# A hybrid encoder layer: Up tiles in one piece of 512 columns, and the order of copies and lows in the turns

## The chip, the core and the metric

The kernel runs on one core of a Trainium2 chip. A core has engines that each work through a queue of their own: TensorE (PE in the profile, its weight loads apart as PEld), VectorE (DVE), ScalarE (ACT), GpSimd (POOL) and SyncE (SP, which here issues transfers only). They synchronise through semaphores. The metric is the device time of one execution in microseconds (us); the median of the runs shown stands for a kernel.

## The reference

One layer over 512 tokens of width 1024, in float32:

```python
x1 = x + rmsnorm(merged @ w_out, g_post_mix)          # merged: retention and SGU branches, gated
h2 = rmsnorm(x1, g_pre_ffn)                           # (512, 1024)
hid = h2 @ w_up                                       # (512, 5632): the Up product
hid = conv3_along_tokens(hid, conv_w) + conv_b        # depthwise
a, b = split(hid, 2)
y = x1 + rmsnorm((gelu(a) * b) @ w_down, g_post_ffn)  # w_down (2816, 1024): the Down product
```

Before it stand the input product (1024 to 8192 columns), a retention in both directions, a spatial gating unit and their output products.

## The kernel before

Every product is made of float32 operands split in two parts of a reduced format, high and low: ScalarE copies the high part (`copy`, line 80), VectorE subtracts it for the low part (line 87, 901). A product is then three matmuls, high x high, high x low, low x high (`mm3`, lines 218 to 221). Activations lie transposed, channels on partitions and the 512 tokens along the free axis; T0 and T1 are the two halves of 256 tokens. A weight block of 128 output channels by 1024 is read from a packed wall in DRAM by SP, split, and kept in one of nine slots (`slot`). The place of a slot's data is chosen by an offset in words: weights of Up blocks lie at 48 (high) and 16 (low) words past the start, activations 64 bytes past a multiple of 256. So Up's weights and its activations differ modulo 256 bytes, as in all stages with 256-wide matmuls but a few small ones; the stages with 512-wide matmuls have weights and activations at one place.

Some products use the Strassen-like scheme of class `Pair`: two output tiles from seven half products of 256 tokens (line 676), 84 matmuls of 256 columns, in three parts. Between the parts ordinary blocks are run, so that the sums on VectorE and ScalarE have time: `gated_pair` does it with two blocks of 512 columns (`f_block`), and the Up product does it in its eight *couples* of tiles, with two `up_block`s. An Up tile is two such blocks (the a and b channels of 128 hidden units each); of the 22 tiles, 0 and 1 are done early (`early`, four blocks), 2, 3, 20 and 21 by plain `up_block`s and 4 to 19 in couples. An `up_block` has 48 matmuls of 256 columns: first the eight k of T0, then, behind `between` (the third part of the Pair), the eight of T1. Early blocks do T0 of all four before T1.

h2 is made four times 128 tokens at a time. `norms(t)` has the residual and two row scales (statistics on ScalarE, a power on POOL, products on VectorE, line 870 to 882); `turn(t)` transposes its 8 pieces on TensorE (line 895) into two PSUM tiles and writes, for each quarter, the high part `h2h` (ScalarE), a raw copy `h2r` (ScalarE) and the low part `h2l` (VectorE). The raw copies serve `h2_sums`, whose results are the Pair's combined inputs. The order in which engines meet these instructions follows from the program's order and a scheduler; the accesses to one PSUM tile are made in program order. turn(0) and turn(1) lie between output products of `Down.finish`, turn(2) behind the first early block, turn(3) behind the fourth.

After Up, `down_forms` builds combined forms of the gated activations (fh, fl, fs, fa) and `products` multiplies them with combined weights, q and t units (dh, dl); `add_whole` handles four plain blocks that are left (`two_parts`, wh, wl). Before the loop over j, seven of the nine forms are built; two come later, in the loop.

Of the kernel before, what the change touches and what calls it, by code (L numbers as in the profile page):

```python
# [10 lines left out]
F32 = mybir.dt.float32  # L11
# [15 lines left out]
NW = 146  # L27
U0, GATE0, GATE1 = 32, 40, 72
LOOK = 4
NBLK = 76  # L30
WARM = 18
RES_OUT = 6
DOWN0 = NW - NF
# [15 lines left out]
def tile_block(ctx: ExitStack, tc, xT, x, wall, par, cs, wsp, bsp, gpost, gpre, gffn, out):  # L49
# [29 lines left out]
    def copy(o, i):  # L79
        nc.scalar.activation(out=o, in_=i, func=AF.Copy)  # L80

    def as32(t):
        return t.bitcast(F32)
# [152 lines left out]
    def col(i):  # L236
        return part[:, i : i + 1]

    xh, xl, xg = [], [], {}

    def load_x(k):
        t = tmp("xT")
        nc.sync.dma_start(t, xT[k])
        h_, l_ = blk(F32R, "xh"), blk(F32R, "xl")
# [598 lines left out]
    def row_scale(q):  # L843
# [7 lines left out]


    gpm, gpf = bcast(gpost, "gpm"), bcast(gpre, "gpr")
    h2h, h2l, h2r = ([[blk(dt, n) for _ in range(4)] for _ in range(2)]
                     for dt, n in ((F32R, "h2h"), (F32R, "h2l"), (F32, "h2r")))
    x1 = [[dp_.tile([P, S], F32, tag=f"x1_{t}{n}", name=f"x1_{t}{n}") for n in range(2)] for t in range(NT)]

    def norms(t, acc):

        xt = halves("x1")  # L860
        for n in range(2):
            nc.sync.dma_start(xt[n], x[t, :, n * S : (n + 1) * S])
        q = small("q", 2, 4)
        for n in range(2):
            mean_square(q, n, acc[n])
        sc, _ = row_scale(q)
        q = small("q", 2, 4)
        for n in range(2):
            z = tmp("z")
            v.scalar_tensor_tensor(  # L870
                out=z, in0=acc[n], scalar=sc, in1=gpm[n], op0=ALU.mult, op1=ALU.mult
            )
            v.tensor_add(xt[n], xt[n], z)
            mean_square(q, n, xt[n])
            nc.gpsimd.dma_start(x1[t][n], xt[n])
            if n == 0 and t in ADDED:
                nc.gpsimd.dma_start(out[t, :, 0:S], xt[0])
        sc, _ = row_scale(q)
        zs = []
        for n in range(2):  # L880
            z = tmp("xn")
            v.scalar_tensor_tensor(
                out=z, in0=xt[n], scalar=sc, in1=gpf[n], op0=ALU.mult, op1=ALU.mult
            )
            zs.append(z)
        return zs

    two = "p (i n) -> p i n"

    def turn(t, zs):  # L890
        g, c = t // 2, slice((t % 2) * P, (t % 2 + 1) * P)
        for n in range(2):
            p = ps()
            for f in range(4):
                nc.tensor.transpose(p[:, f * P : (f + 1) * P], zs[n][:, f * P : (f + 1) * P], ident)
            for i in range(2):
                hi, lo, raw = (h[g][2 * n + i].rearrange(two, i=2)[:, :, c] for h in (h2h, h2l, h2r))
                pf = p[:, 2 * i * P : 2 * (i + 1) * P].rearrange(two, i=2)
                copy(hi, pf)
                copy(raw, pf)  # L900
                v.tensor_sub(lo, pf, as32(hi))  # L901

    def h2(k, t):
        f = slice((k % 2) * 256, (k % 2 + 1) * 256)
        g = t.start // 256
        return h2h[g][k // 2][:, f], h2l[g][k // 2][:, f]

    h2forms = {n: [None] * 4 for n in ("S1", "S2", "S3", "S4")}

# [14 lines left out]
        for n, t in zip(("S1", "S2", "S3", "S4"), (b1, a0, a1, b0)):  # L924
            h2_parts(n, i, t)

    def h2_block(w, o, q):
# [12 lines left out]

    early_w, early_o = [], []

    def early(e, q):

        if q == 0:
            early_w.append(w_get(1))
            early_o.append(ps())
        h2_block(early_w[e], early_o[e], (T0, T1)[q])

    dn_ = Down(mh, ml, KD, RES_OUT)  # L950
    zs = {}
    for t in range(NT):
        acc = [dn_.finish(t, 0)]
        if t > 1:
            turn(t - 2, zs[t - 2])
        acc.append(dn_.finish(t, 1))
        zs[t] = norms(t, acc)
    early(0, 0)
    turn(2, zs[2])
    for e in range(1, EARLY):  # L960
        early(e, 0)
    turn(3, zs[3])
    for e in range(EARLY):
        early(e, 1)

# [20 lines left out]
        gp.append(blk(n="gp"))  # L986
        v.tensor_mul(gp[-1], ca, cb)  # L987

    def two_parts(t):
        h_, l_ = blk(F32R, "fh"), blk(F32R, "fl")  # L990
        split(h_, l_, t)
        return h_, l_

    def down_forms(j):
# [110 lines left out]
        M6: lambda: v.tensor_add(uu, m[M6], e1), M7: after7, M4: after4,  # L1105
    }
    for j in range(DP):
        if j < WHOLE:
            whole.append(two_parts(gp[2 * DP + j]))
        if j % 2 and late:  # L1110
            down_forms(late.pop(0))
        products(m, j, steps if j == DP - 1 else {})
        if j in (3, 5):
            w = w_get()
            for t in range(NT):
                add_whole(m, t, j // 2 - 1, w, j == 5)
            if j == 5:
                copy(c22, m[M8])
# [205 lines left out]
```

## Time and profile before

| | us |
|---|---|
| median of 3 runs (lowest, highest) | 829.57 (828.09, 830.15) |
| profiled execution, its own time | 826.92 |
| its span | 825.1 |
| TensorE busy in it | 814.5 |

A row of the timeline reads: start, duration, engine, line, operation, written tile <- read tiles, shape, count, and in brackets the idle time before it and what ended it. Matmuls are pipelined, so a row's duration is longer than the distance to the next start; the pace is read from starts or from counts in a window. TensorE's records miss a few instructions, and a window counts those that cross its edges.

### The profile page before, as it was taken

How to read it: one execution, taken by the hardware profiler on the slowest of the kernel's cores; microseconds unless marked ns; L12 is line 12 of the kernel's file. 1: busy time of each engine (PE TensorE's matmuls, PEld its weight loads, DVE VectorE, ACT ScalarE, POOL GpSimd, SP SyncE). 2: the span in 40 equal slices, each digit the busy share in tenths (PEclk: the TensorE clock that was granted, in tenths of full speed). 3: DMA queues.
4: the chain of work that ended last, by engine and by line, in shares of the span. 5: the costliest groups of instructions: out<-in, count | busy, mean ns of one | idle time of the engine just before them, and what ended most of it. 6: DMA issues, size and time to landing. Idle time of an engine off the chain costs nothing. (4 is left out here: it accounts for less than half of the span.)

```text
span 825.1 us, 14353 instructions
## 1 busy us (share of the span) xinstructions
PE 814.5 (99%) x5728; PEld 756.6 (92%) x5728; DVE 658.5 (80%) x1076; ACT 429.7 (52%) x733; POOL 104.2 (13%) x108
## 2 busy tenths in 40 slices
PE   9999999999999999999999999999999999999995
PEld 7888888888999999999988899999999999999995
DVE  7489897878898687767765579679899899997956
ACT  6636445536665444444444556456566566644532
POOL 0010000103221111132221201111111100000002
PEclk9999999999999999999999999999999999999999
DMA  8733222213233333233459111333333341243334
GB/s 284 256 116 102 77 77 77 77 52 94 74 105 127 103 103 101 80 101 102 123 173 355 64 54 50 104 102 103 103 103 103 102 155 52 77 141 104 114 129 128
DMA packets 29252, 93.84 MB, mean 114 GB/s; under 512 B 3392, under 2 KB 4032, under 8 KB 29184
## 3 DMA queue, kind: packets, MB, share of 16 engines
q1 hardware_dynamic: 26784, 86.58, 32.5%
q0 software_dynamic: 1968, 6.03, 2.4%
q8 instruction: 45, 0.74, 0.4%
q10 hardware_dynamic: 432, 0.30, 0.1%
q14 instruction: 23, 0.19, 0.1%
HBM read 88.19 MB, written 4.72 MB: 113 GB/s over the span
## 5 line engine op out<-in xcount | busy, mean ns | idle before, releaser
L87 DVE TENSOR_TENSOR wl<-raw,wh 128x1024 fp32r<-128x1024 f32 (+1 forms) x93 | 109.6, 1187 | 49.2 <-PE ps L676 26.5
L80 ACT ACTIVATE wf<-raw 128x512 fp32r<-128x512 f32 x140 | 85.0, 626 | 102.4 <-PE ps L220 42.7
L87 DVE TENSOR_TENSOR wf<-raw,wf 128x512 fp32r<-128x512 f32 x140 | 110.1, 801 | 26.1 <-ACT wf L80 25.4
L220 PE MATMUL ps<-h2l,wh 128*128 128x256 f32 x448 | 123.7, 277 | 0.2 <-DVE h2l L901 0.2
L219 PE MATMUL ps<-h2h,wh 128*128 128x256 f32 x448 | 123.3, 277 | 0.0
L221 PE MATMUL ps<-h2h,wl 128*128 128x256 f32 x448 | 123.3, 276 | 0.0
L676 PE MATMUL ps<-sh,wf 128*128 128x256 f32 x640 | 119.1, 277 | 0.1
L80 ACT ACTIVATE wh<-raw 128x1024 fp32r<-128x1024 f32 (+2 forms) x95 | 93.0, 989 | 35.5 <-DMA raw<-wall 14.0
L676 PEld LDWEIGHTS ps<-sh,wf 128*128 128x128 f32 x640 | 100.7, 188 | 0.8 <-DVE c L704 0.3
L676 PE MATMUL ps<-sl,wf 128*128 128x256 f32 x320 | 88.5, 277 | 0.0
L220 PEld LDWEIGHTS ps<-h2l,wh 128*128 128x128 f32 x448 | 84.0, 188 | 0.7 <-DVE h2l L901 0.7
L219 PEld LDWEIGHTS ps<-h2h,wh 128*128 128x128 f32 x448 | 83.8, 188 | 0.3 <-ACT h2h L80 0.3
L221 PEld LDWEIGHTS ps<-h2h,wl 128*128 128x128 f32 x448 | 83.9, 188 | 0.0
L481 PE MATMUL ps<-wh,xh 128*128 128x512 f32 x192 | 75.0, 391 | 0.0
L482 PE MATMUL ps<-wl,xh 128*128 128x512 f32 x192 | 74.9, 390 | 0.0
L483 PE MATMUL ps<-wh,xl 128*128 128x512 f32 x192 | 74.8, 390 | 0.0
L168 POOL TENSOR_TENSOR raw<-raw,raw 128x512 f32<-128x512 f32 x20 | 34.9, 1743 | 241.0 <-DVE raw L166 217.0
L1062 PE MATMUL ps<-dh,fl 128*128 128x256 f32 x216 | 61.0, 282 | 0.0
L1062 PE MATMUL ps<-dl,fh 128*128 128x256 f32 x216 | 60.3, 279 | 0.5 <-DVE dl L87 0.5
L1062 PE MATMUL ps<-dh,fh 128*128 128x256 f32 x216 | 60.6, 280 | 0.0
L676 PEld LDWEIGHTS ps<-sl,wf 128*128 128x128 f32 x320 | 60.1, 188 | 0.5 <-issue 0.2
L676 PE MATMUL ps<-xh,wf 128*128 128x256 f32 x288 | 53.6, 278 | 0.0
(309 smaller groups left out, 2035.0 us busy)
## 6 DMA issues: line engine op xcount, KB each, us to landing
raw<-wall SPq DMA_DIRECT2D x145, 512.0 KB, 3.6
x<-x SPq DMA_DIRECT2D x22, 256.0 KB, 5.7
xT<-xT SPq DMA_DIRECT2D x8, 256.0 KB, 5.3
x<-x POOLq DMA_DIRECT2D x8, 256.0 KB, 2.4
xT<-xT POOLq DMA_DIRECT2D x4, 256.0 KB, 4.3
out<-zs SPq DMA_DIRECT2D x3, 256.0 KB, 3.4
cs<-cs SPq DMA_DIRECT2D x2, 256.0 KB, 4.0
gpm<-gpost POOLq DMA_DIRECT2D x2, 256.0 KB, 3.7
```

The costliest lines, as they stand in the source:

```text
L80: nc.scalar.activation(out=o, in_=i, func=AF.Copy)
L87: nc.vector.tensor_sub(lo, src, as32(hi))
L168: nc.gpsimd.tensor_tensor(out=w_raw["T2"], in0=w_raw["T1"], in1=w_raw["B22"], op=ALU.add)
L219: nc.tensor.matmul(o, ah, bh, start=start, stop=False)
L220: nc.tensor.matmul(o, ah, bl, start=False, stop=False)
L221: nc.tensor.matmul(o, al, bh, start=False, stop=stop)
L481: nc.tensor.matmul(acc[t], xh[k][:, c], wh[:, f], start=k == 0, stop=False)
L482: nc.tensor.matmul(acc[t], xh[k][:, c], wl[:, f], start=False, stop=False)
L483: nc.tensor.matmul(acc[t], xl[k][:, c], wh[:, f], start=False, stop=k == KD - 1)
L676: nc.tensor.matmul(o, w_[:, c], a_, start=first and k == n == 0, stop=k == 3 and n == 2, skip_group_check=True,)
L1062: nc.tensor.matmul(o, a_[:, c], w_[:, f], start=j == t == i == 0, stop=j == DP - 1 and i == 2 and n not in (M2, M3, M4), skip_group_check= ...
```

## The change

`up_block` runs its eight k over all 512 tokens at once (48 matmuls of 256 columns become 24 of 512), with `between` at the middle k. For that the parts of h2 become tiles of 1024 columns, two k in each, with all 512 tokens side by side (new tag `two`, eight tiles, which x's parts use before and the late forms of Down after); the pool of 512-wide tiles shrinks from 76 to 60, so the memory is the same. The weights of all Up blocks but the first four get offset 0, the activations' place modulo 256 bytes. In `turn` all high and low parts come first and the raw copies after them. The last step of `norms`, `scaled`, is separate, and for the third token tile it is issued behind turn(1)'s lows. turn(3) now lies in the middle of the fourth early block. In the loop of Down the whole blocks' parts are built after the late forms of the same j.

```diff
-NBLK = 76
+NBLK = 60
+    def two(dt=F32R, n="two"):
+        return sb.tile([P, 2 * S], dt, tag="two", bufs=8, name=nm(n))
...
             hi, lo = (slot("wh", 16), slot("wl", 48)) if i >= DOWN0 else (
-                (slot("wh", 48), slot("wl", 16)) if i >= UP0 else (slot("wh"), slot("wl"))
+                (slot("wh", 48), slot("wl", 16)) if UP0 <= i < UP0 + EARLY else (slot("wh"), slot("wl"))
             )
...
-    h2h, h2l, h2r = ([[blk(dt, n) for _ in range(4)] for _ in range(2)]
-                     for dt, n in ((F32R, "h2h"), (F32R, "h2l"), (F32, "h2r")))
+    h2h, h2l = ([two(n=n).rearrange("p (i s) -> p i s", i=2) for _ in range(4)] for n in ("h2h", "h2l"))
+    h2r = [[blk(n="h2r") for _ in range(4)] for _ in range(2)]
...
+        raws = []
         for n in range(2):
...
             for i in range(2):
-                hi, lo, raw = (h[g][2 * n + i].rearrange(two, i=2)[:, :, c] for h in (h2h, h2l, h2r))
-                pf = p[:, 2 * i * P : 2 * (i + 1) * P].rearrange(two, i=2)
+                hi, lo = (h[2 * n + i][:, :, t * P : (t + 1) * P] for h in (h2h, h2l))
+                raw = h2r[g][2 * n + i].rearrange("p (i n) -> p i n", i=2)[:, :, c]
+                pf = p[:, 2 * i * P : 2 * (i + 1) * P].rearrange("p (i n) -> p i n", i=2)
                 copy(hi, pf)
-                copy(raw, pf)
-                v.tensor_sub(lo, pf, as32(hi))
+                low = v.tensor_sub(lo, pf, as32(hi))
+                raws.append((raw, pf))
+        for raw, pf in raws:
+            copy(raw, pf)
+        return low
...
     def up_block(between=None):
-        w, o = w_get(), ps()
-        h2_block(w, o, T0)
-        if between:
-            between()
-        h2_block(w, o, T1)
+        (wh, wl), o = w_get(), ps()
+        for k in range(KD):
+            if between and k == KD // 2:
+                between()
+            c = slice(k * P, (k + 1) * P)
+            mm3(o, wh[:, c], wl[:, c], *h2(k, slice(0, S)), k == 0, k == KD - 1)
         return o
...
         if t > 1:
-            turn(t - 2, zs[t - 2])
+            low = turn(t - 2, zs[t - 2])
+        if t == 3:
+            with tc.issue_after(low.ins):
+                zs[2] = scaled(*xq)
         acc.append(dn_.finish(t, 1))
-        zs[t] = norms(t, acc)
+        xq = norms(t, acc)
+        if t != 2:
+            zs[t] = scaled(*xq)
     early(0, 0)
     turn(2, zs[2])
     for e in range(1, EARLY):
-        early(e, 0)
-    turn(3, zs[3])
+        early(e, 0, (lambda: turn(3, zs[3])) if e == EARLY - 1 else None)
...
-        bh, bl = two_parts(b)
-        sh, sl = two_parts(s_)
-        th, tl = two_parts(a)
+        bh, bl = two_parts(b, j >= EAGER)
+        sh, sl = two_parts(s_, j >= EAGER)
+        th, tl = two_parts(a, j >= EAGER)
...
-        if j < WHOLE:
-            whole.append(two_parts(gp[2 * DP + j]))
         if j % 2 and late:
             down_forms(late.pop(0))
+        if j < WHOLE:
+            whole.append(two_parts(gp[2 * DP + j], j > 1))
```

How the instructions move, at three places. On VectorE around turn(1), before (x, z, qs and xn belong to the norm of the third token tile, h2l to turn(1)):

```order
L873 TENSOR_TENSOR x_844_4735<-x_844_4735,z_4755 128x512
L846 SCALAR_TENSOR_TENSOR qs_4761<-q_4747 128x1
L882 SCALAR_TENSOR_TENSOR xn_4765<-x_843_4734,qr_4762,gpr_4379 128x512
L882 SCALAR_TENSOR_TENSOR xn_4767<-x_844_4735,qr_4762,gpr_4380 128x512
L901 TENSOR_TENSOR h2l_4391<-ps_4787,h2h_4383 128x2x128
L901 TENSOR_TENSOR h2l_4393<-ps_4798,h2h_4385 128x2x128
L901 TENSOR_TENSOR h2l_4392<-ps_4787,h2h_4384 128x2x128
L901 TENSOR_TENSOR h2l_4394<-ps_4798,h2h_4386 128x2x128
```

The four lows come last here. The same place of VectorE with the change:

```order
L875 SCALAR_TENSOR_TENSOR z_4739<-ps_4404,qr_4728,gpm_4368 128x512
L878 TENSOR_TENSOR x_828_4719<-x_828_4719,z_4739 128x512
L908 TENSOR_TENSOR h2l_4379<-ps_4763,h2h_4375 128x2x128
L908 TENSOR_TENSOR h2l_4380<-ps_4763,h2h_4376 128x2x128
L908 TENSOR_TENSOR h2l_4381<-ps_4772,h2h_4377 128x2x128
L908 TENSOR_TENSOR h2l_4382<-ps_4772,h2h_4378 128x2x128
L851 SCALAR_TENSOR_TENSOR qs_4785<-q_4731 128x1
L890 SCALAR_TENSOR_TENSOR xn_4789<-x_827_4718,qr_4786,gpr_4371 128x512
L890 SCALAR_TENSOR_TENSOR xn_4791<-x_828_4719,qr_4786,gpr_4372 128x512
```

The lows of turn(1) stand ahead of the qs and the two xn of the third token tile, behind which they stood before.

On TensorE around turn(3), before (ps_4964 is the fourth early block's output, ps_4861 the first's; ident marks the transposes):

```order
L220 MATMUL ps_4964<-h2l_4394,wh_4531 128x256
L221 MATMUL ps_4964<-h2h_4386,wl_4532 128x256
L219 MATMUL ps_4964<-h2h_4386,wh_4531 128x256
L220 MATMUL ps_4964<-h2l_4394,wh_4531 128x256
L221 MATMUL ps_4964<-h2h_4386,wl_4532 128x256
L895 MATMUL ps_4989<-ident,xn_4857 128x128 x4
L895 MATMUL ps_5000<-ident,xn_4859 128x128 x4
L219 MATMUL ps_4861<-h2h_4387,wh_4513 128x256
L219 MATMUL ps_4908<-h2h_4387,wh_4519 128x256
```

The eight transposes stand between the fourth block and the first reader of their result. The same engine with the change, around the same transposes (ps_4948 is the fourth early block's output):

```order
L222 MATMUL ps_4948<-h2h_4376,wh_4515 128x256
L223 MATMUL ps_4948<-h2l_4380,wh_4515 128x256
L224 MATMUL ps_4948<-h2h_4376,wl_4516 128x256
L902 MATMUL ps_4961<-ident,xn_4841 128x128 x4
L902 MATMUL ps_4970<-ident,xn_4843 128x128 x4
L222 MATMUL ps_4948<-h2h_4377,wh_4515 128x256
L223 MATMUL ps_4948<-h2l_4381,wh_4515 128x256
L224 MATMUL ps_4948<-h2h_4377,wl_4516 128x256
```

The transposes stand in the middle of the fourth early block's first half, twelve matmuls ahead of the first one that reads their result; before, that one followed them directly.

On VectorE at the start of Down, before (dl is the low part of a t or q unit's weights, wl of a whole block's, fl and fa of activation forms):

```order
L87 TENSOR_TENSOR fl_7956<-gp_7571,fh_7955 128x512
L87 TENSOR_TENSOR fa_7959<-gp_7033,fa_7959 128x256
L1000 TENSOR_TENSOR fs_7962<-gp_7033,gp_7044 128x256
L185 TENSOR_TENSOR raw_8117<-raw_8063 128x512
L1001 TENSOR_TENSOR fs_7962<-fs_7962,gp_7033 128x256
L87 TENSOR_TENSOR fl_7968<-gp_7044,fh_7967 128x512
L1002 TENSOR_TENSOR gp_7033<-gp_7033 128x256
L87 TENSOR_TENSOR fl_7972<-fs_7962,fh_7971 128x512
L1003 TENSOR_TENSOR gp_7033<-gp_7044,fs_7962 128x256
L87 TENSOR_TENSOR dl_8008<-raw_8003,dh_8007 128x1024
L87 TENSOR_TENSOR wl_8042<-raw_8039,wh_8041 128x1024
L87 TENSOR_TENSOR fl_7976<-gp_7033,fh_7975 128x512
```

The wl follows the dl directly, and one low of a whole block opens the list. The same place of VectorE with the change (fw are the low parts in the wide tiles):

```order
L1021 TENSOR_TENSOR fs_7366<-fs_7366,gp_6633 128x256
L192 TENSOR_TENSOR raw_7408<-raw_7408,raw_7384 128x256
L1022 TENSOR_TENSOR gp_6633<-gp_6633 128x256
L193 TENSOR_TENSOR raw_7408<-raw_7408,raw_7384 128x256
L1023 TENSOR_TENSOR gp_6633<-gp_6644,fs_7366 128x256
L90 TENSOR_TENSOR fw_7374<-fs_7366,fw_7374 128x512
L188 TENSOR_TENSOR raw_7517<-raw_7467 128x512
L90 TENSOR_TENSOR dl_7413<-raw_7408,dh_7412 128x1024
L90 TENSOR_TENSOR fw_7377<-gp_6633,fw_7377 128x512
L90 TENSOR_TENSOR fl_7381<-gp_7075,fh_7380 128x512
L90 TENSOR_TENSOR fw_7440<-gp_7170,fw_7440 128x512
L90 TENSOR_TENSOR wl_7446<-raw_7443,wh_7445 128x1024
```

The low part of the second whole block's activations (`fl_7956<-gp_7571` before, `fl_7381<-gp_7075` now) moved from before the dl of 1024 columns to behind it, and three lows now stand between that dl and the whole block's wl.

More of the change, by code (lines that the diff above doesn't have):

```diff
@@ L243, in load_x @@
         nc.sync.dma_start(t, xT[k])
-        h_, l_ = blk(F32R, "xh"), blk(F32R, "xl")
+        if k % 2 == 0:
+            xp2.append((two(n="xh"), two(n="xl")))
+        h_, l_ = (a[:, k % 2 * S : (k % 2 + 1) * S] for a in xp2[-1])
         nc.scalar.activation(out=h_, in_=t, func=AF.Copy, scale=col(PRE + k))
@@ L896, in turn @@
             for i in range(2):
-                hi, lo, raw = (h[g][2 * n + i].rearrange(two, i=2)[:, :, c] for h in (h2h, h2l, h2r))
-                pf = p[:, 2 * i * P : 2 * (i + 1) * P].rearrange(two, i=2)
+                hi, lo = (h[2 * n + i][:, :, t * P : (t + 1) * P] for h in (h2h, h2l))
+                raw = h2r[g][2 * n + i].rearrange("p (i n) -> p i n", i=2)[:, :, c]
+                pf = p[:, 2 * i * P : 2 * (i + 1) * P].rearrange("p (i n) -> p i n", i=2)
                 copy(hi, pf)
-                copy(raw, pf)
-                v.tensor_sub(lo, pf, as32(hi))
+                low = v.tensor_sub(lo, pf, as32(hi))
[3 more added lines that the diff above has]
+        return low
     def h2(k, t):
-        f = slice((k % 2) * 256, (k % 2 + 1) * 256)
-        g = t.start // 256
-        return h2h[g][k // 2][:, f], h2l[g][k // 2][:, f]
+        return tuple(h[k // 2][:, k % 2, t] for h in (h2h, h2l))
     h2forms = {n: [None] * 4 for n in ("S1", "S2", "S3", "S4")}
@@ L925, in h2_sums, with h2_block @@
             h2_parts(n, i, t)
-    def h2_block(w, o, q):
+    def h2_block(w, o, q, between=None):
         wh, wl = w
         for k in range(KD):
+            if between and k == KD // 2:
+                between()
             c = slice(k * P, (k + 1) * P)
@@ L933, in up_block, with early @@
     def up_block(between=None):
-        w, o = w_get(), ps()
-        h2_block(w, o, T0)
-        if between:
-            between()
-        h2_block(w, o, T1)
+        (wh, wl), o = w_get(), ps()
+        for k in range(KD):
+            if between and k == KD // 2:
+                between()
+            c = slice(k * P, (k + 1) * P)
+            mm3(o, wh[:, c], wl[:, c], *h2(k, slice(0, S)), k == 0, k == KD - 1)
         return o
     early_w, early_o = [], []
-    def early(e, q):
+    def early(e, q, between=None):
         if q == 0:
@@ L947, in early @@
             early_o.append(ps())
-        h2_block(early_w[e], early_o[e], (T0, T1)[q])
+        h2_block(early_w[e], early_o[e], (T0, T1)[q], between)
     dn_ = Down(mh, ml, KD, RES_OUT)
@@ L987, in gated, with two_parts @@
         v.tensor_mul(gp[-1], ca, cb)
-    def two_parts(t):
-        h_, l_ = blk(F32R, "fh"), blk(F32R, "fl")
+    def two_parts(t, wide=False):
+        if wide:
+            w = two(n="fw")
+            h_, l_ = w[:, :S], w[:, S:]
+        else:
+            h_, l_ = blk(F32R, "fh"), blk(F32R, "fl")
         split(h_, l_, t)
```

5 lines of the change are left out of this document (3 added, 2 removed).

## The prediction

> **What bounds the kernel now.** I read the page first (busy shares and granted clock), then what TensorE waits for, then the pace of its matmuls by windows, then the timeline at the three places where it loses time near the change.
>
> ```profile
> span 825.1 us, 14353 instructions
> PE 814.5 (99%) x5728; PEld 756.6 (92%) x5728; DVE 658.5 (80%) x1076; ACT 429.7 (52%) x733; POOL 104.2 (13%) x108
> PEclk9999999999999999999999999999999999999999
> PE ps L1062 <- DVE dl L87: 0.5, 1, 0.5
> PE ps L220 <- DVE h2l L901: 0.2, 1, 0.2
> PEld ps L220 <- DVE h2l L901: 0.7, 2, 0.4
> ```
>
> TensorE is busy 99% of the span at full clock, and the waits that the trace lists for it near the change are single ones of under 1 us. The time is therefore the number of matmuls times their pace, plus a few small holes. Only something that alters the pace, or one of those holes, can move it.
>
> **The pace.** Windows (us busy, instructions, clock) over a stretch of 512-wide matmuls and over the Up product, then one period of a gated pair (256-wide Pair products and two 512-wide blocks) and one period of an Up couple (the same, with its blocks as 256-wide halves):
>
> ```profile
> 100.00:150.00 50.00, 50.00 (x282) 43.83 (x281) 43.46 (x72) 25.41 (x36) 1.20 (x2) 1.00 0.24 83
> 500.00:550.00 50.00, 50.00 (x444) 50.00 (x443) 41.77 (x63) 26.30 (x44) 7.46 (x5) 1.00 0.30 96
> 454.87 0.39 PE L830 MATMUL ps<-wh,mh 128*128 128x512 f32 x1
> 455.78 0.39 PE L831 MATMUL ps<-wl,mh 128*128 128x512 f32 x1
> 364.81:385.31 20.50, 20.50 (x133) 18.56 (x132) 15.34 (x21) 9.45 (x16) 5.99 (x4) 1.00 0.35 105
> 518.44:538.84 20.40, 20.40 (x182) 20.40 (x181) 13.21 (x21) 11.03 (x19) 3.41 (x2) 1.00 0.31 101
> L220 PE MATMUL ps<-h2l,wh 128*128 128x256 f32 x448 | 123.7, 277 | 0.2 <-DVE h2l L901 0.2
> L221 PE MATMUL ps<-vh,sm 128*128 128x256 f32 x32 | 9.1, 283 | 0.0
> ```
>
> The Up couple has 84 + 96 = 180 matmuls of 256 columns in 20.40 us: 113.3 ns each (the windows count a few that cross their edges). The four steps from 454.87 to 455.78 are 0.91 us, 227 ns for 512 columns: twice 113.3. So TensorE already takes columns at full rate in the Up product, although weight loads fill its load side there (50.00 of 50.00, against 43.83 at 512 columns). The gated pair has 84 matmuls of 256 and 48 of 512. At those paces they take 84 x 0.1133 + 48 x 0.2267 = 20.40 us, and the trace has 20.50.
>
> **The change, part by part. 1. Widening.** 24 Up blocks x 48 = 1152 matmuls of 256 columns become 576 of 512, and 576 weight loads go. By the rows above, two of 113.3 ns become one of 226.7 ns: 0.0 us, with an uncertainty of about 1 ns a pair (rounding of the timeline over four steps), 0.6 us either way. The removed weight loads lie beside the matmuls and are worth nothing while the pace is that of columns. The 512-wide blocks get weights at the activations' place (64 bytes past a multiple of 256), as the 512-wide stage at 454 us has it; the 256-wide groups with both operands at one place (vh,sm) show 283 ns busy against 277, so for 256 columns that place costs some 6 ns, and I take it to be harmless for 512 because of the 227 ns. What I do charge is the alternation: each Up couple now has the form of the gated pair, which takes 0.10 us more than its columns. Eight couples: +0.8 us (bounds: 0, if the switches are covered, and 1.6, twice the row).
>
> The Trainium skill ("TensorE: Matmul & The Clock Gate", section "Back-to-back issue gap") gives a lone matmul 262 cycles at 256 columns and 518 at 512, so a pair would save 6 cycles; as an estimate from that page 576 x 2.5 ns = 1.4 us, and the sum below would be -1.8 in place of -0.43. The trace's 113.3 and 227 show no such fixed part, and the measurement decides. The skill's "SBUF — State Buffer" (section "Who interferes with whom") lists the reads of moving operand and weights as independent ports, by which the placement would matter to nothing; the 283 against 277 does not agree.
>
> **2. turn(1) and the first early block.** PE, VectorE and ScalarE there (464.04 is a low of turn(0), for its duration):
>
> ```profile
> 471.62 0.28 PE L219 MATMUL ps<-h2h,wh 128*128 128x256 f32 x1
> 471.93 0.39 PE L220 MATMUL ps<-h2l,wh 128*128 128x256 f32 x1
> 473.07 0.39 PE L220 MATMUL ps<-h2l,wh 128*128 128x256 f32 x1 [0.19 <-DVE h2l L901]
> 475.12 1.04 PE L895 MATMUL ps<-ident,xn 128*128 128x128 f32 x8
> 470.12 1.41 DVE L882 SCALAR_TENSOR_TENSOR xn<-x,qr,gpr 128x512 f32<-128x512 f32 x2 [0.74 <-POOL qr L849]
> 471.46 0.74 DVE L901 TENSOR_TENSOR h2l<-ps,h2h 128x256 fp32r<-128x256 f32 x2
> 464.04 0.42 DVE L901 TENSOR_TENSOR h2l<-ps,h2h 128x256 fp32r<-128x256 f32 x1 [0.72 <-ACT h2r L80]
> 472.60 0.98 DVE L901 TENSOR_TENSOR h2l<-ps,h2h 128x256 fp32r<-128x256 f32 x2 [0.39 <-ACT h2r L80]
> 469.36 0.37 ACT L80 ACTIVATE h2h<-ps 128x256 fp32r<-128x256 f32 x1
> 471.90 0.38 ACT L80 ACTIVATE h2h<-ps 128x256 fp32r<-128x256 f32 x1 [1.33 <-DVE h2l L901]
> ```
>
> The early block's 24 matmuls take 475.12 - 471.62 = 3.50 us, where 24 x 0.1133 = 2.72. The missing 0.78 is the wait for h2l: VectorE does xn of the next token tile first (470.12 to 471.53) and only then turn(1)'s lows; each low of a transposed tile also waits for the raw copy ahead of it, and the next h2h for that low (471.90). In the changed order the lows come behind ScalarE's first copies (three of the four h2h need nothing else and were done by 469.73 before) and xn behind them. Four lows of about 0.4 us from there, the last behind two raw copies and one more h2h, give some 471.4, and its first reader is the 19th matmul, at 471.62 + 18 x 0.1133 = 473.66. Value taken: -0.78; bounds -0.78 and 0. What is late next is xn(2): qs, the power (0.74) and the two products (1.41) then end at about 473.7, and turn(2)'s transposes come at 471.62 + 2.72 = 474.34. It holds by 0.6 us.
>
> **3. turn(3) inside the last early block.**
>
> ```profile
> 475.92 0.36 PE L219 MATMUL ps<-h2h,wh 128*128 128x256 f32 x1
> 475.91:484.55 8.64, 8.64 (x75) 1.00 0.16 61
> 484.55 1.03 PE L895 MATMUL ps<-ident,xn 128*128 128x128 f32 x8
> 485.62 0.86 PE L219 MATMUL ps<-h2h,wh 128*128 128x256 f32 x5
> 487.39 0.28 PE L219 MATMUL ps<-h2h,wh 128*128 128x256 f32 x1
> 485.19 0.38 ACT L80 ACTIVATE h2h<-ps 128x256 fp32r<-128x256 f32 x1 [3.19 <-PE ps L895]
> ```
>
> Before, the time to the next matmul behind the transposes is 485.62 - 484.55 = 1.07 us where turn(2)'s is 475.92 - 475.12 = 0.80, and the 14 matmuls from there to 487.39 take 1.77 us where 14 x 0.1133 = 1.59: together 0.45 us of waiting for the first copies. With 12 matmuls (1.4 us) between the transposes and their first reader that wait is gone: -0.45. From the start of the transposes ScalarE's first h2h begins 0.64 later (485.19) and takes 0.38, and a low takes 0.42: 1.44, against a first reader of the low at 0.80 + 12 x 0.1133 + 0.11 = 2.27. So the 12 matmuls suffice. But there is a second pace. The 72 matmuls after turn(2) (475.91 to 484.55) run at 120 ns, not 113.3, and 113.3 is back only behind turn(3)'s wait. Without that wait I expect the 96 matmuls of the second early halves to keep 120 ns: 96 x 6.7 ns = +0.64. The two give +0.19 (bounds -0.45 and +0.19). I take +0.19: the nearest row is turn(2)'s, behind which nothing waited either.
>
> **4. The start of Down.** PE there, VectorE, the chain that ended last (start, us, what) and VectorE's share of the window before:
>
> ```profile
> 720.82 0.28 PE L1062 MATMUL ps<-dh,fh 128*128 128x256 f32 x1
> 721.58 0.39 PE L1062 MATMUL ps<-dl,fh 128*128 128x256 f32 x1 [0.48 <-DVE dl L87]
> 724.52 0.28 PE L1079 MATMUL ps<-wl,fh 128*128 128x256 f32 x1
> 719.38 0.68 DVE L87 TENSOR_TENSOR fl<-fs,fh 128x512 fp32r<-128x512 f32 x1
> 721.45 1.22 DVE L87 TENSOR_TENSOR wl<-raw,wh 128x1024 fp32r<-128x1024 f32 x1
> 700.00:720.00 20.00, 20.00 (x37) 1.00 0.23 79
> 605.63 0.33 DVE c L693
> 720.39 1.15 DVE dl L87
> 721.58 2.98 PE ps L1062 x23
> ```
>
> PE reaches the fourth t unit at 720.82 + 0.12 = 720.94 and gets its dl at 721.58: 0.64 us late. The chain behind it is VectorE's from 605.63 on, and VectorE is full in the last 20 us. So here VectorE sets the end, and what TensorE gains or loses before is taken up: its arrival moves by -0.78 + 0.19 + 0.80 = +0.21, which the hole of 0.64 absorbs. dl itself moves with the start of that chain (605.63 lies after half of the couples: -0.78 + 0.19 + 4 x 0.10 = -0.19) and by the edit of Down: one 512-wide low (0.60 from start to start) of the second whole tile now stands behind dl. So dl comes 0.19 + 0.60 = 0.79 earlier, at 720.79, and TensorE, at 721.15, no longer waits. Its matmul of 721.58 comes at 721.15: -0.43 for the whole. Bounds: without the 0.60, 721.39, -0.19; with the couples' switches at nothing, TensorE at 720.35 and dl at 720.40, about -1.2. The whole block's wl now stands three lows behind dl instead of directly behind it: dl ends at 720.79, three lows (3 x 0.60) give 722.6, wl itself (1.14 before the next) 723.7, and its first reader now comes at 724.52 - 0.43 = 724.1. It holds by 0.4 us; if two more lows slip ahead, it misses by 0.8, which is the bound.
>
> **Edits at nothing.** x's parts, h2's and the wide forms change buffers, not their number. One wait is new: the first wide form of Down takes the buffer of the first h2 part, so ScalarE waits there until the last Up block has passed its second k, 6 x 0.227 = 1.4 us after its start. Ahead of it on ScalarE lies the conv copy that starts with that block, and behind it two more parts and the gelu of the last tile, for which VectorE waits:
>
> ```profile
> 680.69 0.67 ACT cv L971
> 680.00:700.00 20.00, 19.74 (x36) 1.00 0.18 54
> ```
>
> That copy covers 0.67 of the 1.4; the remaining 0.7 is hidden while VectorE has other work (19.74 of 20.00 there) and would move dl by up to 0.7 if it had none, of which 0.4 is TensorE's own distance from dl (721.15 against 720.79). I take nothing; bound +0.3. At the start of the kernel the same loads and copies are issued in another order; bound 0.3 either way.
>
> **Sum** against the profiled execution (826.92, 825.1 in its span): 0.0 (columns) + 0.80 (alternation) - 0.78 (turn 1) + 0.19 (turn 3) - 0.64 (hole at Down taken up) = -0.43, so 826.5. The median of the runs shown is 829.57, 2.65 above the profiled one; against it 829.1.
>
> **The rivals.**
> (a) *The slow pace costs more than the profile shows, and 512 columns cure it.* If the 2.65 us between the median and the profiled execution are Up matmuls that ran at 120 ns (1152 x 6.7 ns = 7.7 us if all did), the change removes them: 829.57 - 2.65 - 0.43 = 826.5. For it: the second pace exists, in a stretch where the load side has no slack (50.00 of 50.00). Against it: the profiled execution shows it nowhere in Up beyond turn(3).
> (b) *Slower: the switch from 512 back to 256 columns sets the second pace.* Then the 84 Pair matmuls of each couple run at 120 ns: 8 x 84 x 6.7 ns = +4.5 us: 829.57 - 0.43 + 4.5 = 833.6. It decides from the first couple on. Against it: the gated pairs have the same switches and take 20.50, not 21.06.
> (c) *VectorE late at Down.* wl misses by its bound of 0.8 and the hole of 0.64 stays: 829.57 - 0.43 + 1.44 = 830.6, no change by measurement. For it: VectorE is full for 40 us ahead of that place; against it: the spare of 0.4.
> (d) *The turns do not do what they say:* the tiles' copies still wait for one another, and the 0.78 stays in part or whole: 829.57 + 0.35 = 829.9 at most.
>
> **How the numbers follow.** Forecast (terms as taken) 0.52, (a) 0.22, (b) 0.09, (c) 0.09, (d) 0.08. A measurement of this kernel tells a change from none at about 0.3%, 2.5 us. The forecast, (c) and (d) lie inside; (a) lies at its edge, beyond it with 0.8 of its chance; (b) beyond on the other side. For what of the forecast could hide in executions slower than the profiled one I move 0.09 to faster and 0.05 to slower: faster 0.27, same 0.59, slower 0.14. The likeliest case alone is 828.3 to 830.5; the range reaches to (a) and part of the way to (b): 825.6 to 831.4.
>
> **What would show it.** A couple's period of 20.50 (step 1; 20.40 says no switch cost, 21 and more says (b)); 512-wide Up matmuls at 227 ns; the first early block in 2.72 us; transposes of turn(3) without a hole and the pace behind them (120 or 113.3); no wait for dl or wl at Down. The prediction is wrong if 512-wide Up matmuls run above 227 ns, or if the time moves by more than 2.5 us without one of these rows moving.

## The result, and the profile after

The changed kernel takes 826.04 us (median of 5 executions, 825.85 to 826.34), the kernel before 829.57 (827.54 to 830.15): a ratio of 0.9962 with a 95% interval of 0.9948 to 0.9975. It is 3.5 us faster, 0.43%. That lies in the forecast range, but 3.1 below the time named as likeliest, and just beyond the 0.3% that were to count as a change. The profiled executions differ by far less: 825.93 against 826.92, spans 824.2 and 825.1. Most of the gain is therefore not between the two profiles. It is the scatter of the kernel before: its executions cover 2.6 us, those of the changed one 0.5. Where the median of such scattered executions falls is partly luck. In the four later groups of the kernel before (below) it lies between 827.08 and 828.96; over all its 84 executions it is 827.48, and over 12 of the changed kernel 825.89. By these medians the change is worth some 1.6 us; 3.5 is against the five executions that were drawn first.

The page after, what TensorE waits for, and the chain that ended last:

```profile
span 824.2 us, 13203 instructions
PE 814.3 (99%) x5152; PEld 734.4 (89%) x5152; DVE 658.4 (80%) x1076; ACT 430.6 (52%) x733; POOL 104.2 (13%) x108
PE 97%; issue 1%; DVE 1%; POOL 1%; DMA 0%; POOLq 0%; ACT 0%; ACTq 0%; DVEq 0%
PE ps L1082 <- DVE dl L90: 0.2, 1, 0.2
```

576 matmuls are gone, TensorE's busy time is the same, and VectorE has nearly left the chain that ended last (1%). The same line of the page before:

```profile
DVE 11%; PE 11%; issue 2%; POOL 1%; ACT 1%; DMA 0%; POOLq 0%; DVEq 0%; SPq 0%
```

TensorE's windows after (us busy, instructions, clock, DMA): one period of an Up couple, the second early halves, a stretch of 512-wide Up:

```profile
517.84:538.34 20.50, 20.50 (x134) 1.00 0.28 92
484.00:495.00 11.00, 11.00 (x95) 1.00 0.24 73
681.00:701.00 20.00, 20.00 (x90) 1.00 0.17 50
```

The couple takes 20.50 us, as the gated pairs do. The early halves run at about 119 ns a matmul (11.00 for some 92 or 93, the window's edges left out), and 512 columns at 227 (20.00 for 88). The timeline at the three places:

```profile
471.58 0.28 PE L222 MATMUL ps<-h2h,wh 128*128 128x256 f32 x1
474.31 0.71 PE L902 MATMUL ps<-ident,xn 128*128 128x128 f32 x5
470.07 0.76 DVE L908 TENSOR_TENSOR h2l<-ps,h2h 128x256 fp32r<-128x256 f32 x2 [0.78 <-ACT h2h L83]
471.49 0.42 DVE L908 TENSOR_TENSOR h2l<-ps,h2h 128x256 fp32r<-128x256 f32 x1 [0.67 <-ACT h2h L83]
472.73 1.41 DVE L890 SCALAR_TENSOR_TENSOR xn<-x,qr,gpr 128x512 f32<-128x512 f32 x2 [0.75 <-POOL qr L854]
482.31 1.03 PE L902 MATMUL ps<-ident,xn 128*128 128x128 f32 x8
483.11 0.36 PE L222 MATMUL ps<-h2h,wh 128*128 128x256 f32 x1
720.46 0.27 PE L1082 MATMUL ps<-dh,fh 128*128 128x256 f32 x1
720.89 0.39 PE L1082 MATMUL ps<-dl,fh 128*128 128x256 f32 x1 [0.16 <-DVE dl L90]
719.62 1.22 DVE L90 TENSOR_TENSOR dl<-raw,dh 128x1024 fp32r<-128x1024 f32 x1
723.84 0.38 PE L1099 MATMUL ps<-wl,fh 128*128 128x256 f32 x1
724.06 0.28 PE L1099 MATMUL ps<-wh,fl 128*128 128x256 f32 x1
```

The first early block takes 474.31 - 471.58 = 2.73 us, its hole of 0.78 is gone. turn(3)'s transposes are followed without a wait (483.11 - 482.31 = 0.80). At Down's dl 0.31 of the 0.64 us are left, and the whole block's wl is 0.1 late (0.22 from 723.84 to the next).

### The profile page after: what moved, and what is told of

Same layout as the page of the kernel before. It is cut to its first block, busy times and chain, and to the rows that moved or that the text cites. A ratio compares the mean times of both kernels' runs of the same rounds, so it can differ in the third digit from the quotient of the medians.

```text
span 824.2 us, 13203 instructions
## 1 busy us (share of the span) xinstructions
PE 814.3 (99%) x5152; PEld 734.4 (89%) x5152; DVE 658.4 (80%) x1076; ACT 430.6 (52%) x733; POOL 104.2 (13%) x108
## 4 chain that ended last, share of the span: by engine, by line
PE 97%; issue 1%; DVE 1%; POOL 1%; DMA 0%; POOLq 0%; ACT 0%; ACTq 0%; DVEq 0%
PE ps L681 23%; PE ps L223 13%; PE ps L222 12%; PE ps L224 12%; PE ps L1082 11%; PE ps L486 5%; PE ps L487 5%; PE ps L488 5%; PE ps L835 2%; PE ps L836 2%; PE ps L837 2%; PE ps L1099 2%; PE ps L760 1%; PE ps L286 1%; PE ps L611 0%
## 5 line engine op out<-in xcount | busy, mean ns | idle before, releaser
L223 PE MATMUL ps<-h2l,wh 128*128 128x512 f32 (+1 forms) x256 | 93.1, 363 | 0.0
L222 PE MATMUL ps<-h2h,wh 128*128 128x512 f32 (+1 forms) x256 | 93.0, 363 | 0.0
L224 PE MATMUL ps<-h2h,wl 128*128 128x512 f32 (+1 forms) x256 | 92.5, 361 | 0.0
L224 PEld LDWEIGHTS ps<-h2h,wl 128*128 128x128 f32 x256 | 48.0, 188 | 7.7
L222 PEld LDWEIGHTS ps<-h2h,wh 128*128 128x128 f32 x256 | 48.1, 188 | 6.9
L223 PEld LDWEIGHTS ps<-h2l,wh 128*128 128x128 f32 x256 | 48.0, 188 | 6.6
L83 ACT ACTIVATE dh<-raw 128x768 fp32r<-128x768 f32 (+1 forms) x36 | 34.0, 948 | 30.7 <-PE ps L1082 15.4
L1082 PE MATMUL ps<-dh,fl 128*128 128x256 f32 x168 | 47.3, 281 | 0.0
L1082 PE MATMUL ps<-dh,fh 128*128 128x256 f32 x168 | 47.2, 281 | 0.0
```

The lines of the kernel that those rows point to most:

```text
L222: nc.tensor.matmul(o, ah, bh, start=start, stop=False)
L223: nc.tensor.matmul(o, ah, bl, start=False, stop=False)
L224: nc.tensor.matmul(o, al, bh, start=False, stop=stop)
L1082: nc.tensor.matmul(o, a_[:, c], w_[:, f], start=j == t == i == 0, stop=j == DP - 1 and i == 2 and n not in (M2, M3, M4), skip_group_check= ...
```

## The experiments

The theory to be tested was rival (a), called P: executions of the kernel before that take longer than the profiled one run part of their 256-wide matmuls at the second pace. Its rival V: VectorE's chain to Down is longer in them. The kernel before was run beside each group on the same chip, and its medians there were 827.50 (first group, one chip), 827.23 (second) and 828.96 (third; both of these on another chip). Its executions lay between 826.1 and 830.1 each time.

**The kernel before, again.** No edit.

> The kernel before, unchanged, once more, to see where an execution of 828 to 830 us loses what the profiled one of 826.92 did not. Theory P (pace): part of the 256-wide matmuls of the Up product run at about 120 ns in place of 113.3; a profile above 828 shows Up windows of 50 us with fewer than 444 instructions (425 at 120 ns). Theory V (VectorE): Up keeps 113.3 ns and the hole at the start of Down, 0.64 us in the profiled execution, is 2 to 4 us, with VectorE full ahead of it. Median 829.0 to 830.0 by both.

Median 827.08 (825.92 to 830.24), ratio 0.9994 (0.9981 to 1.0007); both theories had expected 829.0 to 830.0, and the median missed that. The execution that was profiled took 829.57, the median of the first comparison. TensorE's windows of the profiled execution of 826.92 and its timeline at the sixth couple, then the same of this one:

```profile
560.00:600.00 40.00, 40.00 (x355) 1.00 0.33 102
640.00:670.00 30.00, 30.00 (x267) 1.00 0.47 141
680.00:700.00 20.00, 20.00 (x178) 1.00 0.18 54
636.74 0.28 PE L676 MATMUL ps<-h2h,wf 128*128 128x256 f32 x1
637.09 0.38 PE L676 MATMUL ps<-sh,wf 128*128 128x256 f32 x1
```

```profile
span 827.8 us, 14353 instructions
560.00:600.00 40.00, 40.00 (x355) 1.00 0.32 100
600.00:630.00 30.00, 30.00 (x267) 1.00 0.35 116
640.00:670.00 30.00, 30.00 (x254) 1.00 0.42 126
680.00:700.00 20.00, 20.00 (x171) 1.00 0.18 55
637.32 0.28 PE L676 MATMUL ps<-h2h,wf 128*128 128x256 f32 x1
637.68 0.39 PE L676 MATMUL ps<-sh,wf 128*128 128x256 f32 x1
```

Up to 630 us the counts are equal. At 637.3 TensorE waits a quarter of a microsecond in the third part of the sixth couple's Pair (0.36 from start to start). The execution of 826.92 has the same hole (0.35 at 636.74) and goes on at 113.3 ns; here, from there to Down 30 us hold 254 matmuls in place of 267, 5% fewer: the second pace, 118.9 ns from start to start in place of 113.3. 589 matmuls lie between there and Down; 589 x 5.6 ns = 3.3 us. Down's hole of 0.64 is not in this execution, since TensorE comes later than dl. 3.3 - 0.64 = 2.7, against 829.57 - 826.92 = 2.65. That the two agree so well is partly chance: this execution is 0.57 late already at the first early block (472.19 against 471.62), and it makes up about as much in Down and behind its last matmul. P holds for this execution, and V does not: there is no larger hole. In the other slow executions of this kernel no profile shows the pace; their times alone are in keeping with an entry at different couples.

**The change without its turns.** Raw copies between the parts, the third norm's end and turn(3) in their old places:

```diff
                 copy(hi, pf)
-                low = v.tensor_sub(lo, pf, as32(hi))
-                raws.append((raw, pf))
+                copy(raw, pf)
+                v.tensor_sub(lo, pf, as32(hi))
...
-        early(e, 0, (lambda: turn(3, zs[3])) if e == EARLY - 1 else None)
+        early(e, 0)
+    turn(3, zs[3])
```

> The change without its turns: Up in one piece of 512 columns and the new order in Down, but raw copies between the high and low parts, the third norm's last step in its old place, turn(3) behind the fourth early block. P: the spread of the executions is gone (within 0.6 us) and the time is that of the change plus the hole of turn(1) and of turn(3) minus the second pace behind turn(3): 826.04 + 0.78 - 0.19 = 826.6. V: the same, since the order in Down is the new one.

826.40 (825.76 to 826.91), ratio 0.9984 (0.9974 to 0.9994). The scatter shrinks to 1.2 us with the old turns (0.6 was expected): it goes with the new Up, not with the turns. The time is within 0.2 of the expected one, for a partly different reason: the second pace set in here too behind turn(2), but ended by itself, without a wait, within some seven matmuls (8 us hold 73 instructions, not 70):

```profile
476.00:484.00 8.00, 8.00 (x73) 1.00 0.17 66
```

**The change without width and place.** Up in halves, weights at their old offsets, everything else new:

```diff
-                (slot("wh", 48), slot("wl", 16)) if UP0 <= i < UP0 + EARLY else (slot("wh"), slot("wl"))
+                (slot("wh", 48), slot("wl", 16)) if i >= UP0 else (slot("wh"), slot("wl"))
...
     def up_block(between=None):
-        (wh, wl), o = w_get(), ps()
-        for k in range(KD):
-            if between and k == KD // 2:
-                between()
-            c = slice(k * P, (k + 1) * P)
-            mm3(o, wh[:, c], wl[:, c], *h2(k, slice(0, S)), k == 0, k == KD - 1)
+        w, o = w_get(), ps()
+        h2_block(w, o, T0)
+        if between:
+            between()
+        h2_block(w, o, T1)
         return o
```

> The change with Up in halves of 256 columns and weights at the place they had before; turns and the order in Down are the new ones. P: the spread stays, median 828.0 to 829.5, and the profile is either near 825.5 (Up at 113.3 ns) or shows the second pace in Up. V: the spread is gone and the time is that of the change without the couples' 0.10 each: 825.2 to 826.0. A third way: the second pace behind turn(3) now goes on into tiles 2 and 3 and further, since no 512-wide matmul ends it: up to 826.04 + 192 x 6.7 ns = 827.3, and more if it goes on into the couples.

835.23 (834.51 to 835.55), ratio 1.0086 (1.0069 to 1.0104): slower than the kernel before by 8 us. It is the third of the expected ways, gone much further than the 827.3 that it began with. The windows of an early couple and of the later ones:

```profile
520.00:540.00 20.00, 20.00 (x170) 1.00 0.22 66
560.00:600.00 40.00, 40.00 (x339) 1.00 0.34 106
640.00:670.00 30.00, 30.00 (x255) 1.00 0.32 94
```

The second pace that is there from turn(2) on lasts through all couples to Down in the profiled execution, and the small scatter (1.0 us) suggests the same of the others. 1152 matmuls of Up blocks and 672 of the Pairs at 5.6 ns more are 10.2 us; without the couples' switches (8 x 0.10) that is 9.4 more than the changed kernel, measured 9.2. So the new turns, without width and place, would have been a loss.

**The same, with turn(3) behind the fourth early block.**

```diff
-        early(e, 0, (lambda: turn(3, zs[3])) if e == EARLY - 1 else None)
+        early(e, 0)
+    turn(3, zs[3])
```

> As the halves before (256 columns, new turns, new order in Down: 835.2 us with the second pace of 118.9 ns from turn(2) to Down), but turn(3) behind the fourth early block again, so that TensorE waits there some 0.4 us. Theory W (a wait ends the pace): 113.3 ns from turn(3) on, until some later hole sets the second pace again: 825.5 to 829.5, spread like that of the kernel before. Theory T (the new turns as such): 118.9 ns to Down as before, 835.

826.74 (825.30 to 829.48), ratio 0.9993 (0.9980 to 1.0007). Windows of the profiled execution, one of 828.93:

```profile
486.00:494.00 8.00, 8.00 (x73) 1.00 0.23 68
560.00:600.00 40.00, 40.00 (x355) 1.00 0.33 102
640.00:670.00 30.00, 30.00 (x255) 1.00 0.46 140
```

One edit that puts turn(3) back, and with it gives TensorE back a wait of some 0.4 us, takes 8.5 us away. The scatter is back too (4.2 us), so neither the new turn(1) nor the new order in Down is what removes it. Behind that wait the pace is 113.3 ns (x355 in 40 us), and behind the hole of the sixth couple it is 118.9 again (x255 in 30). So a short wait can end the second pace, and can set it. Theory W stands, with that addition; which of the two a wait does is not settled. The edit also moves the transposes from the middle of a block to its end, and no run keeps their place and changes the wait alone, so that it is the wait is argued and not shown.

**512 columns with the weights at the other place.**

```diff
-                (slot("wh", 48), slot("wl", 16)) if UP0 <= i < UP0 + EARLY else (slot("wh"), slot("wl"))
+                (slot("wh", 48), slot("wl", 16)) if i >= UP0 else (slot("wh"), slot("wl"))
```

> The change with the weights of all Up blocks at 48 and 16 words past the slot's start, so in another place than the activations modulo 256 bytes. If the place costs nothing at 512 columns: 826.0 and 227 ns a matmul. If the wrong place costs as much as at 256 columns, 6 ns a matmul: 826.0 + 576 x 6 ns = 829.5 and 233 ns.

831.33 (831.16 to 832.17), ratio 1.0043 (1.0028 to 1.0057).

```profile
687.00:707.00 20.00, 20.00 (x87) 1.00 0.15 50
640.00:670.00 30.00, 30.00 (x197) 1.00 0.37 123
497.00:517.00 20.00, 20.00 (x89) 1.00 0.20 60
517.80:522.80 5.00, 5.00 (x46) 1.00 0.35 123
522.84 0.28 PE L681 MATMUL ps<-sh,wf 128*128 128x256 f32 x1
522.95 0.39 PE L222 MATMUL ps<-h2h,wh 128*128 128x512 f32 x1
```

In the couples the 512-wide matmuls take 233.2 ns from start to start, and the Pairs between them 119. It did not begin so: the 96 wide matmuls of tiles 2 and 3 took 229.0 ns, and the first 48 of the Pair behind them ran at 113.6. With the first wide block of the couples (522.95) both became slower, without a hole (0.11 from the start ahead of it). So wide matmuls at the other place did end the second pace once, but did not keep it away. It lives on at 512 columns, where it costs about as many nanoseconds a matmul as at 256 (6.5 and 5.6).

**256 columns with the weights at the activations' place.** The change with `up_block` in halves, the slots as in the change.

> The halves with all Up weights but the early ones at the activations' place modulo 256 bytes, so the change without its width. If that place by itself keeps 256 columns at 113.3 ns: 825.5. If 256 columns at one place always run at 119 to 120 ns (the mean busy of 283 against 277 ns in small groups of the kernel before): 1152 x 6 ns more than 113.3, the Pair products staying as they fall: 832.5 to 835.5, with no spread.

832.71 (831.95 to 833.53), ratio 1.0065 (1.0051 to 1.0078). A Pair stretch of the first couple, and a stretch of Up blocks alone:

```profile
519.00:524.00 5.00, 5.00 (x47) 1.00 0.40 129
688.00:708.00 20.00, 20.00 (x169) 1.00 0.09 28
```

The Up blocks run at 120.0 ns from start to start in every couple, but the Pair between them at 113.3, and no scatter of the old kind is left (1.6 us). So at one place 256 columns take 120 ns in every Up block, and behind them the second pace is over. 1152 x 6.7 ns - 0.8 us of switches = 6.9, measured 832.71 - 826.04 = 6.7 (7.2 against the 825.54 of the changed kernel on this chip, below). Place ends the second pace and keeps it away, and width hides what the place costs: with the new turns the four combinations are 835.23 (neither), 831.33 (width), 832.71 (place) and 826.04 (both).

**Width and place in the plain tiles alone.** The couples' blocks in halves at the old offsets (`up_halves` is the `up_block` of before):

```diff
-            o = [up_block()]
+            o = [up_halves()]
             p.part2()
-            o.append(up_block(p.part3))
+            o.append(up_halves(p.part3))
```

> The change with the couples' blocks in halves of 256 columns (weights at the place of before), 512 columns only in tiles 2, 3, 20 and 21. If a 512-wide stretch at one place ends the second pace: couples begin at 113.3 ns, period 20.40, and a hole at about 635 us can set the pace anew: 825.3 in the best executions, up to 829 in others. If it does not end it: 118.9 ns in the couples, 833.

825.21 (823.45 to 827.88), ratio 0.9978 (0.9966 to 0.9991). In the profiled execution (824.77) the 96 wide matmuls of tiles 2 and 3 end the pace, and the couples hold 113.3 ns to their end:

```profile
560.00:600.00 40.00, 40.00 (x355) 1.00 0.32 101
640.00:670.00 30.00, 30.00 (x267) 1.00 0.46 141
635.61 0.28 PE L681 MATMUL ps<-h2h,wf 128*128 128x256 f32 x1
635.95 0.39 PE L681 MATMUL ps<-sh,wf 128*128 128x256 f32 x1
```

The hole in the sixth couple is there (0.34 from start to start), and this time it sets no second pace. Five of the twelve executions are above 826.6, so in others something presumably does.

**Another place for the early blocks and Down.** Their weights at 32 words, 192 modulo 256 bytes, high and low.

> The change with the weights of the early blocks and of Down (high and low) at 192 modulo 256 bytes, activations at 64 as before. Down runs at 117.8 ns a matmul and the early blocks at 120 behind turn(2) in the change. If a place of its own for both parts is what 113.3 ns needs: Down 900 x 4.5 ns = -4 us, early -1.1 us, 821 to 822. If the pace of Down comes from its stationary operand changing two times in three matmuls or from the turn, not from the place: 826.0.

825.96 (825.63 to 827.16), ratio 0.9987 (0.9978 to 0.9995); the changed kernel has 825.54 on this chip (below). Down takes 118.7 ns in place of 117.8, and the early blocks stay at 119. A third place is not what they lack; why Down never reaches 113.3 is open.

**Wide only where needed, and the early blocks.** The kernel with wide plain tiles, and the second blocks of the last four couples wide too; then that one with the second early block's weights at the activations' place and this block first in the second halves; the changed kernel beside them.

```diff
-            o.append(up_halves(p.part3))
+            o.append((up_block if i >= 12 else up_halves)(p.part3))
...
-    for e in range(EARLY):
+    for e in (1, 0, 2, 3):
         early(e, 1)
```

> The change unchanged, on the chip of the next two, as their yardstick: 825.9 to 826.2, spread within 1 us.

> 512 columns in tiles 2, 3, 20 and 21 and, in the last four couples, in the second block alone (the one with the Pair's third part in its middle); all other blocks of the couples in halves at the place of before. If matmuls with weights at the activations' place end the second pace, whatever set it, the hole at 635 us no longer costs more than itself: best time of the kernel with wide plain tiles (823.45) + 4 x 0.05 us of switches, 823.3 to 825.0, spread within 1.2 us. If they do not, the spread stays at 823.5 to 828.

> As the one before, and the weights of the second early block at the activations' place too, with that block first in the second early half. If matmuls of 256 columns at one place end the second pace as well, behind turn(2) only its 24 matmuls and behind turn(3) the twelve left and its 24 run at 120 ns, the other 36 + 72 at 113.3: 108 x 6.6 ns = 0.7 us less than the one before, 822.6 to 824.3. If the width is what ends it: no change against the one before, and 120 ns in all of the early blocks.

On this chip the changed kernel took 825.54 (825.17 to 826.24; ratio 0.9962, 0.9948 to 0.9975), the first variant 825.71 (825.24 to 826.20; 0.9968, 0.9953 to 0.9982) and the second 824.92 (824.77 to 825.89; 0.9956, 0.9941 to 0.9972). The first keeps the scatter small, as expected of a kernel that ends the pace behind the sixth couple's hole, but its time is 0.7 above the whole range that was expected (823.3 to 825.0), and it is no better than the change. The second shows what the trick at the early blocks does; windows behind turn(2) and behind turn(3), of the changed kernel and of this variant:

```profile
474.50:482.30 7.80, 7.80 (x68) 1.00 0.19 70
483.10:496.00 12.90, 12.90 (x111) 1.00 0.25 83
```

```profile
474.00:482.00 8.00, 8.00 (x72) 1.00 0.18 68
482.80:495.00 12.20, 12.20 (x109) 1.00 0.24 80
```

The 60 matmuls behind turn(2) take 7.04 us in place of 7.21, and the 108 behind turn(3) 12.50 in place of 12.93: 0.6 us, expected 0.7. Behind turn(2) the 24 matmuls at one place take 120 ns and those behind them 113.3. So 256-wide matmuls at one place end the pace as wide ones do. Its median is 0.6 below that of the change, the best median of a kernel here, though also above the range expected (822.6 to 824.3); one group of runs carries that 0.07%, and the executions of the two overlap.

## Why the prediction was right, and where not

- **Widening, 0.0 for the columns and +0.10 a couple:** right. 512 columns take 227 ns, the couple 20.50 us.
- **turn(1), -0.78:** right, 2.73 us in place of 3.50. xn(2) ended at 474.1 and was in time for the transposes at 474.31, with 0.2 to spare and not 0.6.
- **turn(3), +0.19:** right. The second pace itself is 118.9 ns; the 120 of the prediction has the slow first step behind the transposes in it. From turn(2)'s transposes to the first couple there are 517.84 - 474.31 = 43.53 us, 518.44 - 475.12 = 43.32 before: +0.21.
- **Down, -0.64:** half right. dl ended at 720.8 as worked out, but TensorE came earlier than the sum had it, so 0.31 of the hole is left. What was missing is a hole that I did not price: the third part of the sixth couple loses 0.46 us over its 24 matmuls in the kernel before (3.18 us, where 24 x 0.1133 = 2.72), and in the change it doesn't wait (2.73). The profiled times differ by 0.99 us, where the sum gave 0.43: -0.77 (turn 1) + 0.21 (turn 3) + 0.80 (couples) - 0.46 (this hole) - 0.33 (Down) = -0.55, and the rest is a hole of 0.15 at 763.9 us that only the profile before has, 0.04 ahead of the first early block, and 0.25 behind the last matmul, which I cannot put down to the change. wl came 0.1 late; the spare of 0.4 was used up by the same shift.
- **The step that failed is the last one: "The median of the runs shown is 829.57, 2.65 above the profiled one; against it 829.1."** It carried the 2.65 over to the changed kernel as if it were an offset of the measurement. It was rival (a)'s: second-pace matmuls in executions that the profile had not caught, as the one profile of 829.57 shows; for the rest of them that is argued from the scatter, which ends with the new Up. The measured 3.53 is these 2.65, the 0.99 between the profiles and -0.11 (the changed kernel's median above its profiled execution); that is how the gain divides, and no test of it. (a) had 826.5, measured 826.04; its chance of 0.22 was too low. So the time is inside the range because the range was drawn to reach (a); the forecast's own sum, 829.1, did not come. How far off it looks is partly the luck of the first five executions of the kernel before. The argument against it, that the profiled execution shows the pace nowhere in Up beyond turn(3), leaned on one execution that was faster than all five timed ones.
- **Rival (a)'s cure was half of it.** It let the width end the second pace. By the runs it is the weights' place that ends it for good (832.71 and 113.3 ns in the Pairs), and the width that makes this place free. Width alone ended it once, in tiles 2 and 3, lost it again in the first couple, and gives 831.33.
- **Rival (b)**, the pace set by each switch back to 256 columns, did not come: 113.5 ns in the Pairs behind 512 columns. With the weights at the other place the Pairs do run at 119 ns, but there the pace came with a switch from 256 to 512 columns (522.95), and the switch back before it (517.5) left 113.6.
- What I took for a fault of the new turn(3), +0.19, has its true price where nothing ends the pace: 8.5 us between the two kernels with halves. Width and place carry the change: without the turns they give 826.40, while the turns without them lose 8 us.

For the two paces the runs have no mechanism. The rows of the weight loads do not tell them apart; here they are at 113.3 ns (before, 560 to 600 us), at 118.9 (halves at the other place, 560 to 600) and at 120.0 (halves at one place, 688 to 708):

```profile
L219 PEld LDWEIGHTS ps<-h2h,wh 128*128 128x128 f32 x64 | 12.0, 188 | 0.0
L222 PEld LDWEIGHTS ps<-h2h,wh 128*128 128x128 f32 x61 | 11.5, 188 | 0.0
L222 PEld LDWEIGHTS ps<-h2h,wh 128*128 128x128 f32 x56 | 10.8, 192 | 0.0
```

A load's row is 188 ns in both paces and 192 for halves at one place. The Trainium skill ("TensorE: Matmul & The Clock Gate", section "LDWEIGHTS (loading the stationary operand)") gives a weight load of 128 columns as 128/1.2 = 107 ns. The rows are longer than that, but they overlap (188 ns each at 113.3 from start to start), so they do not test it. As an estimate from that page, a 256-wide matmul of 113 ns would leave a load 6 ns of slack, and a 512-wide one 120. The halves at one place lose 6.7 ns a matmul, and the wide ones at one place none, which would fit a load that has become some 10 ns longer. But the rows show 4 ns and not 10, and at the other place the wide ones lose 6.5 as well, where there is slack enough; that doesn't fit. No run here shows the length of a load by itself.

## What to carry to other kernels

When the executions of a kernel scatter by more than the change could be worth, profile it again until one near the median is caught, and compare the counts of matmuls in equal windows. A pace that depends on what ran before can be 5% slower at full clock and 99% busy, so neither the busy share nor the list of waits shows it. A wait that is removed may have been what ended such a stretch; test each part of a change without the others.

## What was not expected of the hardware

- One and the same stream of 256-wide matmuls runs at 113.3 or 118.9 ns from start to start, for hundreds of microseconds, at a granted clock of 1.00. The slower pace began behind transposes, behind a hole of a quarter of a microsecond, and once with neither, at a switch to 512 columns with the weights at the other place. It ended behind turn(3) where TensorE waited there (0.45 us in the kernel before), and once by itself.
- The place of the weights against the activations modulo 256 bytes matters in two ways: at one place the 256 columns of Up take 120.0 ns and 512 columns 226.7, and behind either the slower pace was over in every run that had them. At different places 512 columns took 229.0 at first and then 233.2.
- The same hole at the same matmul set the slower pace in one execution of the kernel before (829.57) and not in another (826.92).
